# One layer of a hybrid RWKV-7 / RG-LRU block on one core: a score product moved up, a scan moved back, and the head norm's products and first gating regrouped

## The chip, the core and the metric

The kernel runs on one core of a Trainium2 chip. The time is the device time of one execution in microseconds (us). Profile times are microseconds on the clock of one profiled execution unless they are marked ns. The engines are PE (TensorE, the matrix products), DVE (VectorE), ACT (ScalarE), POOL (GpSimd) and SP (SyncE, which here only issues transfers). PEld is PE's weight load.

## What is computed

One layer at sequence length 512 and width 1024, all in float32. A normed input is projected by `w_in` (1024 x 4864) and feeds two mixers side by side; their outputs are gated, summed and projected, then follow a cross-attention and a gated conv-FFN. What the change touches lies in the two mixers and where they meet:

```python
def rwkv7_recurrence(r, decay, k, v, a, b):
    def step(state, inp):
        sa = jnp.einsum('bhij,bhj->bhi', state, a_t)
        state = (state * w_t[:, :, None, :] + sa[..., None] * b_t[:, :, None, :]
                 + v_t[..., None] * k_t[:, :, None, :])
        y_t = jnp.einsum('bhij,bhj->bhi', state, r_t)
...
    y = ((y - mean) * lax.rsqrt(var + LNX_EPS)).reshape(bsz, s, A_WIDTH) * lnx_g + lnx_b
    bonus = jnp.sum(r * k * r_k, axis=-1, keepdims=True) * v
    return (y + bonus.reshape(bsz, s, A_WIDTH)) * g
...
    u = xb * gate_x * mult
    _, h = lax.associative_scan(_lin_combine, (a, u), axis=1)
    return h * jax.nn.gelu(py.astype(jnp.float32))
...
        y_a = rwkv7_branch(...) @ w_branch_a[l]
        y_b = rglru_branch(...) @ w_branch_b[l]
        merged = (jax.nn.sigmoid(proj[..., cb2:cg1]) * y_a
                  + jax.nn.sigmoid(proj[..., cg1:]) * y_b)
        x = x + merged @ w_mix_out[l]
```

## The kernel before, in words

**Products in split float32.** Each float32 operand is split into a high part in a rounded format and a low part, and one product is made of three (`mm3`, L239): high by high, high by low, low by high. The weights stream from memory in tiles of 128 x 1024 (512 KB): SP issues the load (L169, four buffers), ACT casts the high part (`win_h`, L182, three buffers), DVE subtracts to get the low part (`win_l`, L183, three buffers), and PE uses both. A block of the input projection (`in_ps0` to `in_ps37`, 128 x 512) is 48 products of 128 x 256; three PSUM buffers serve these blocks. The same streaming serves `wbb` (weights of YB's branch) and `wba` (of the recurrence's branch).

**Order.** PE's order is the string `ORDER` (L44 on), which `Products.arrange` turns into dependencies: `in_ps25:42 sc3 in_ps25` puts 42 products of block 25, then all of `sc3`, then the rest of the block. On DVE, ACT and SP the build's scheduler chooses the order from the program order, priorities and the dependencies, so a change on PE moves instructions there too; each engine then runs its list in order.

**Recurrence.** It works in chunks of 64 steps. For each pair of heads, `prep2` makes the decayed keys `KBt` and the tile `AK` (L725 is the last write of `KBt`); `scores` (L753 on) makes the products `sc` of a chunk with itself, which DVE masks into `AK` (L767) and `BZ` (L768) and ACT copies into `BZ` (L769); four transfers per pair write the triangles to memory (`dM`, L774). There are four pairs, `sc0` to `sc3`. After the last pair two transfers bring all triangles back as `Nm` (L836), and a triangular inverse is built on DVE: 31 steps of a product `zz` (L843) and a sum into `Zt` (L845), each step's tile one column wider, up to 31 x 31, then a copy `Zn` (L846). `Zt` is cleared first (L837); it lies in the memory of the pool that `prep2` used, so the clearing has to wait for what still reads there, among it the transfer of `pr` to `dBo` (L733). While this inverse runs, PE works through the blocks 26 to 37 (`gate_block`) and the bonus sums `bo` (`bs` on DVE, L742).

**Chunk steps.** `chunk(c)` (c = 0 to 7) carries the state: PE makes `x`, DVE copies `Xs` (L949), PE makes `u`, ACT and DVE copy it into `UV` (L961, L962), PE makes `s` and `y`, DVE makes `Sn` (L978), adds it into the next `UV` (L982; `states[c]` is this instruction) and makes `SP` (L990). Between these steps PE works on the blocks 14 to 21.

**The other mixer** (`px_gates`, `px_scan`) makes four blocks of a gated linear scan in the same stretch: per block a DVE product (L1057), a one-column clear (L1058), a product (L1059) and the scan (L1060). Scans 2 and 3 are issued as a pair.

**The meeting point.** The recurrence's output is normed per head in two halves of time, each in two pairs (`group_norm`, tiles `gv0_0` to `gv1_1`): ACT squares, the square is split (`gv_h` on ACT L234, `gv_l` on DVE L235, in memory slots with the tag "xb"), PE sums it with `bonesr`, ACT takes the inverse root, DVE multiplies (L1019), scales and adds the bonus (L1022), gates (L1023) and splits into `ya`. YB's branch `yb_ps0` to `yb_ps7` (L1101 on) comes first on PE; each result is gated on DVE into `mB` (L1106) with a gate block `gb` loaded from memory (L1103, tags "ga", "gx", "st" in turn, two slots each). `yb_ps3` takes the PSUM buffer of `yb_ps0`, so it waits for `mB` of block 0. Then `ya_ps0` to `ya_ps7`, the mixing projection, attention and FFN follow.

Of the kernel before, what the change touches and what calls it, by code (L numbers as in the profile page):

```python
# [9 lines left out]
F32 = mybir.dt.float32  # L10
F32R = mybir.dt.float32r
AF = mybir.ActivationFunctionType
ALU = mybir.AluOpType
# [4 lines left out]
P = 128  # L18
T = 512
# [23 lines left out]

ORDER = """  # L44
in_ps4 in_ps5 psw0 psa0 in_ps0 in_ps1:6 ss0 in_ps1 in_ps8 in_ps9:6 sc0 in_ps9 psw1 psa1 ss1 in_ps6 in_ps7 in_ps2:12 sc1 in_ps2
psw2 psa2 in_ps3:10 ss2 in_ps3 in_ps10 in_ps11:36 sc2 in_ps11 in_ps22 psw3 psa3 ss3 in_ps23 in_ps24 in_ps25:42 sc3 in_ps25
in_ps26 in_ps27 in_ps28 bo0 in_ps29 bo1 in_ps30 bo2 in_ps31 bo3 in_ps32 in_ps33 in_ps34 in_ps35 in_ps36 in_ps37
in_ps14:40 zh0 in_ps14 in_ps15:14 zo0 zh16 in_ps15:16 zo16 in_ps15:8 vr0 ga0 in_ps15:6 x0 y0:8 kbr0 in_ps15
in_ps16:8 u0 vr1 gx0 in_ps16:12 s0 y0 kbr1 ga1 in_ps16:12 x1 y1:8 gx1 in_ps16:12 u1 vr2 in_ps16 in_ps17:8 s1 y1 kbr2
in_ps17:12 x2 y2:8 in_ps17:12 u2 vr3 in_ps17:12 s2 y2 kbr3 in_ps17 in_ps18:8 x3 y3:8 ga2 in_ps18:12 u3 vr4 gx2  # L50
in_ps18:12 s3 y3 kbr4 ga3 in_ps18:12 x4 y4:8 gx3 in_ps18 in_ps19:8 u4 vr5 in_ps19:12 s4 y4 kbr5 gv0_0 in_ps19:12 x5
y5:8 in_ps19:12 u5 vr6 gg0_0 in_ps19 in_ps20:8 s5 y5 kbr6 in_ps20:12 x6 y6:8 gv0_1 in_ps20:12 u6 vr7 gg0_1
in_ps20:12 s6 y6 kbr7 in_ps20 in_ps21:8 x7 y7:8 in_ps21:12 u7 in_ps21:12 y7 gg1_0 gg1_1 in_ps21 yb_ps0:18 yb_ps1:8 gv1_0 gv1_1 yb_ps1:10 yb_ps0 yb_ps1
yb_ps2 yb_ps3 yb_ps4 yb_ps5 yb_ps6 yb_ps7 ya_ps0 ya_ps1 ya_ps2 ya_ps3 ya_ps4 ya_ps5 ya_ps6 ya_ps7 mix_ps0
mix_ps1 mix_ps2 mix_ps3 mix_ps4 mix_ps5 mix_ps6 mix_ps7 q_ps0_0:32 rxc_ps q_ps0_0 q_ps0_1 q_ps1_0:24 sc_ps0_0
sc_ps0_1 q_ps1_0 q_ps1_1:4 sc_ps0_2 prT_ps0:2 q_ps1_1:8 sc_ps0_3 prT_ps0:2 q_ps1_1:18 prT_ps0 q_ps1_1:10 o_ps0
# [25 lines left out]
def hybrid_block_kernel(ctx: ExitStack, tc: tile.TileContext, xT_d, mT_d, pv_d, cst_d, win_d, wk_d, wv_d,  # L82
                        lup_d, gup_d, rga_d, rgx_d, wba_d, wbb_d, wmix_d, wq_d, wo_d, wfi_d, wfo_d, out_d):
    nc = tc.nc
    V, S = nc.vector, nc.scalar
# [144 lines left out]
    def sum_exact(ps, blocks, src, pool, tag, name, bufs=2, pin=lambda ins: ins):  # L230

        hi = pool.tile(list(src.shape), F32R, tag=tag, name=f"{name}_h", bufs=bufs)
        lo = pool.tile(list(src.shape), F32R, tag=tag, name=f"{name}_l", bufs=bufs)
        S.copy(hi, src)  # L234
        V.tensor_tensor(lo, src, hi.bitcast(F32), ALU.subtract)  # L235
        pin(PE.matmul(ps, blocks, hi, start=True, stop=False))
        PE.matmul(ps, blocks, lo, start=False, stop=True)
# [47 lines left out]
    bonesr = cp.tile([P, P], F32R, name="bonesr")  # L285
# [73 lines left out]
    with tc.tile_pool(name="p0", bufs=1, reuse_waits="tile") as p0:  # L359
# [102 lines left out]
        st = stream(wv_d, "wv", at=OFF)  # L462
# [162 lines left out]
    tp = tp_ctx.enter_context(tc.tile_pool(name="tp", bufs=1, reuse_waits="tile"))  # L625
# [195 lines left out]
    for k, i in enumerate(IN_REST[NEARLY:NMID]):  # L821
        gate_block(i - 22)
        j = k + NEARLY - 6
# [81 lines left out]
    yT = vT  # L905
# [32 lines left out]
    states, uvs = [], []  # L938
# [61 lines left out]
    ya2 = pa.tile([P, 2, 4, T], F32R, tag="AR", name="ya2")  # L1000


    def group_norm(hf, jp, ps, psg):
        n = T // 2
        ts = slice(hf * n, (hf + 1) * n)
        js = slice(2 * jp, 2 * jp + 2)
        nm = f"{hf}_{jp}"
        bo = ch.tile([P, 2, n], F32, tag="bo", name=f"bo{nm}", bufs=2)
        nc.scalar.dma_start(bo, dBo[js, :, ts].rearrange("j p t -> p j t"))
        y2 = ch.tile([P, 2, n], F32, tag="y2", name=f"y2{nm}", bufs=2)  # L1010
        S.activation(y2, yT[:, js, ts], AF.Square)
        p3 = ps.rearrange("p (j t) -> p j t", j=2)
        sum_exact(ps, bonesr, y2.rearrange("p j t -> p (j t)"), tp, "xb", f"gv{nm}")
        tab.rsqrt(y2, p3, 1.0 / HD, eps[:, 1:2])
        g3 = psg.rearrange("p (j t) -> p j t", j=2)
        for i in range(2):
            j = 2 * jp + i
            PE.matmul(g3[:, i, :], gup[:, j * P:(j + 1) * P], sgx[:, ts], start=True, stop=True)
        V.tensor_tensor(y2, yT[:, js, ts], y2, ALU.mult)  # L1019
        for i in range(2):  # L1020
            j = 2 * jp + i
            V.scalar_tensor_tensor(y2[:, i, :], y2[:, i, :], par("lnx_g", j), bo[:, i, :], ALU.mult, ALU.add)  # L1022
        V.tensor_tensor(yT[:, js, ts], y2, g3, ALU.mult)  # L1023
# [28 lines left out]
    def px_scan(b, xb, ga, gx, behind):  # L1052
        tab(ga, ga, AF.Exp, scale=c8[:, b:b + 1])
        tab(gx, gx, AF.Ln, bias=eps[:, 2:3])
        tab(gx, gx, AF.Exp, scale=0.5)
        with tc.issue_after(behind.ins) if behind is not None else nullcontext():
            V.scalar_tensor_tensor(gx, ga, 1.0, gx, ALU.add, ALU.mult)  # L1057
        V.memset(gx[:, 0:1], 1.0)  # L1058
        V.tensor_tensor(xb, xb, gx, ALU.mult)  # L1059
        V.tensor_tensor_scan(YB[:, b, :], ga, xb, 0.0, ALU.mult, ALU.add)  # L1060
# [9 lines left out]
    for i in IN_REST[NMID:]:  # L1070
        if i < 18:
            pair.append(px_gates(i - 14))
            if len(pair) == 2:
                for p in pair:
                    px_scan(*p, {1: states[2]}.get(p[0]))
                pair = []
        elif i < 22:
            if i == 18:
                for jp in range(2):
                    group_norm(0, jp, rw_ps(f"gv0_{jp}", prg, "rg"), rw_ps(f"gg0_{jp}", prg, "rg"))  # L1080
            py_block(i - 18)
        else:
            gate_block(i - 22)
# [10 lines left out]
    mB = big.tile([P, KB, T], F32, tag="act16_1", name="mB")  # L1094
# [4 lines left out]
            V.tensor_tensor(yb2[:, 1, b, :], yb, yb2[:, 0, b, :].bitcast(F32), ALU.subtract)  # L1099
    ub = Units(wbb_d, "wbb", at=OFF)  # L1100
    for m in range(KB):  # L1101
        gb = tp.tile([P, T], F32, tag=("ga", "gx", "st")[m % 3], name=f"gb{m}", bufs=2)
        nc.sync.dma_start(gb, dG[8 + m])  # L1103
        psb = mm_ps(f"yb_ps{m}")
        dense(psb, ub, lambda kb: (yb2[:, 0, kb, :], yb2[:, 1, kb, :]), 4)
        V.tensor_tensor(mB[:, m, :], psb, gb, ALU.mult)  # L1106
    pq_ctx.close()
    tp_ctx.close()

# [550 lines left out]
```

## Time and profile before

| | before |
|---|---|
| time, median of 3 runs | 878.45 us (873.0 to 879.46) |
| profiled execution | 876.36 us, span 874.6 us, granted clock 0.997 |
| PE busy | 853.7 us (98%) |
| DVE busy | 677.3 us (77%) |
| ACT busy | 511.3 us (58%) |
| POOL busy | 132.6 us (15%) |
| DMA | 201.60 MB, mean 231 GB/s |

A row of the timeline has a start, a duration, the engine, the line, the operation with output and inputs, a count, and in brackets the idle time of the engine before it with what ended it; the duration of a row with a count covers the first start to the last end. Matmuls overlap, so the step from one row's start to the next tells more than a duration. `SPq` and `ACTq` rows are the issue of a transfer, not the transfer; the time to landing stands in the view of a tile. The waits of an engine are summed per line and releaser. Names of tiles leave the number of the buffer out: `in_ps` is any of the blocks.

### The profile page before, as it was taken

How to read it: one execution, taken by the hardware profiler on the slowest of the kernel's cores; microseconds unless marked ns; L12 is line 12 of the kernel's file. 1: busy time of each engine (PE TensorE's matmuls, PEld its weight loads, DVE VectorE, ACT ScalarE, POOL GpSimd, SP SyncE). 2: the span in 40 equal slices, each digit the busy share in tenths (PEclk: the TensorE clock that was granted, in tenths of full speed). 3: DMA queues.
4: the chain of work that ended last, by engine and by line, in shares of the span. 5: the costliest groups of instructions: out<-in, count | busy, mean ns of one | idle time of the engine just before them, and what ended most of it. 6: DMA issues, size and time to landing. Idle time of an engine off the chain costs nothing.

```text
span 874.6 us, 19292 instructions
## 1 busy us (share of the span) xinstructions
PE 853.7 (98%) x7884; PEld 825.9 (94%) x7884; DVE 677.3 (77%) x1096; ACT 511.3 (58%) x786; POOL 132.6 (15%) x163
## 2 busy tenths in 40 slices
PE   9999999999999999999999999999999999999996
PEld 8899999998988888999999899999999999999996
DVE  6896988759836787585575568799888888999774
ACT  7777666534337667234464457666666566768563
POOL 0111123021002221001122211111111111111100
PEclk9999999999999999999999999999999999999998
DMA  8888799687676898648887858999999999998953
GB/s 288 309 286 201 191 239 219 217 234 229 197 191 133 198 241 204 200 161 234 222 237 175 194 146 194 259 274 291 285 258 288 306 280 291 261 291 224 299 178 97
DMA packets 97576, 201.60 MB, mean 231 GB/s; under 512 B 19600, under 2 KB 30992, under 8 KB 97424
## 3 DMA queue, kind: packets, MB, share of 16 engines
q1 hardware_dynamic: 62240, 118.57, 40.5%
q0 software_dynamic: 25504, 67.38, 37.3%
q10 hardware_dynamic: 9744, 14.42, 5.0%
q8 instruction: 62, 1.02, 0.4%
q14 instruction: 26, 0.21, 0.1%
HBM read 188.54 MB, written 78.12 MB: 305 GB/s over the span
## 4 chain that ended last, share of the span: by engine, by line
PE 74%; DVE 13%; ACT 6%; DMA 4%; issue 3%; DVEq 0%; ACTq 0%; SPq 0%
PE fx_ps L97 14%; PE in_ps L97 12%; PE fyz_ps L97 10%; PE ox_ps L97 7%; PE oyz_ps L97 5%; PE co_ps L97 5%; PE mix_ps L97 4%; PE q_ps L97 4%; PE yb_ps L97 2%; DVE win_l L183 2%; PE v_ps L97 2%; PE o_ps L97 1%; DVE zz L843 1%; PE sc_ps L97 1%; DVE Zt L845 1%
## 5 line engine op out<-in xcount | busy, mean ns | idle before, releaser
L97 PE MATMUL in_ps<-hT,win_h 128*128 128x256 f32 x1216 | 211.8, 278 | 0.0
L97 PEld LDWEIGHTS in_ps<-hT,win_h 128*128 128x128 f32 x1216 | 184.8, 188 | 3.6 <-issue 1.9
L97 PE MATMUL in_ps<-hT,win_l 128*128 128x256 f32 x608 | 174.1, 286 | 3.5 <-DVE win_l L183 3.5
L97 PEld LDWEIGHTS in_ps<-hT,win_l 128*128 128x128 f32 x608 | 114.2, 188 | 7.4 <-DVE win_l L183 4.7
L206 ACT CAST wfi_h<-wfi_r 128x1024 fp32r<-128x1024 f32 x77 | 80.9, 1051 | 68.6 <-PE fyz_ps L97 22.8
L563 POOL DMA_DIRECT2D dS<-in_wfi x66 | 66.7, 1039 | 332.9 <-PE in_ps L97 136.8
L207 DVE TENSOR_TENSOR wfi_l<-wfi_r,wfi_h 128x1024 fp32r<-128x1024 f32 x77 | 94.1, 1222 | 19.8 <-ACT wfi_h L206 19.8
L599 POOL DMA_DIRECT2D dOs<-in_wfo x54 | 39.8, 799 | 169.1 <-PE fx_ps L97 66.1
L97 PE MATMUL fx_ps<-hq,wfi_h 128*128 128x256 f32 x352 | 61.2, 276 | 0.0
L97 PE MATMUL fx_ps<-hr,wfi_h 128*128 128x256 f32 x352 | 61.1, 276 | 0.0
L97 PE MATMUL fyz_ps<-hq,wfi_h 128*128 128x256 f32 x352 | 61.1, 276 | 0.0
L183 DVE TENSOR_TENSOR win_l<-win_r,win_h 128x1024 fp32r<-128x1024 f32 x38 | 46.3, 1222 | 18.3 <-ACT win_h L182 18.1
L97 PE MATMUL ox_ps<-go,wfo_h 128*128 128x256 f32 x352 | 59.9, 276 | 0.0
L182 ACT CAST win_h<-win_r 128x1024 fp32r<-128x1024 f32 x38 | 39.8, 1047 | 30.1 <-PE in_ps L97 24.8
L1467 DVE TENSOR_TENSOR wfo_l<-wfo_r,wfo_h 128x1024 fp32r<-128x1024 f32 (+1 forms) x39 | 47.3, 1216 | 11.0 <-ACT wfo_h L1466 10.9
L1466 ACT CAST wfo_h<-wfo_r 128x1024 fp32r<-128x1024 f32 (+1 forms) x39 | 40.4, 1037 | 24.6 <-PE ox_ps L97 8.7
L97 PEld LDWEIGHTS fx_ps<-hr,wfi_h 128*128 128x128 f32 x352 | 53.0, 188 | 0.2 <-ACT sn L1402 0.2
L97 PEld LDWEIGHTS fx_ps<-hq,wfi_h 128*128 128x128 f32 x352 | 53.2, 188 | 0.0
L97 PEld LDWEIGHTS ox_ps<-go,wfo_h 128*128 128x128 f32 x352 | 53.1, 188 | 0.0
L97 PEld LDWEIGHTS fyz_ps<-hq,wfi_h 128*128 128x128 f32 x352 | 53.0, 188 | 0.0
L97 PE MATMUL fyz_ps<-hq,wfi_l 128*128 128x256 f32 x176 | 48.7, 277 | 0.6 <-DVE wfi_l L207 0.6
L97 PE MATMUL fx_ps<-hq,wfi_l 128*128 128x256 f32 x176 | 48.6, 276 | 0.0
(392 smaller groups left out, 2331.2 us busy)
## 6 DMA issues: line engine op xcount, KB each, us to landing
dS<-in_wfi POOLq DMA_DIRECT2D x66, 512.0 KB, 8.0
wfi_r<-dS SPq DMA_DIRECT2D x44, 512.0 KB, 6.9
win_r<-in_win SPq DMA_DIRECT2D x38, 512.0 KB, 5.2
wfi_r<-in_wfi SPq DMA_DIRECT2D x33, 512.0 KB, 7.2
dS<-dS POOLq DMA_DIRECT2D x22, 512.0 KB, 5.6
dOs<-in_wfo POOLq DMA_DIRECT2D x12, 512.0 KB, 8.4
wk_r<-in_wk SPq DMA_DIRECT2D x8, 512.0 KB, 5.1
wv_r<-in_wv SPq DMA_DIRECT2D x8, 512.0 KB, 4.9
```

The lines of the kernel that those rows point to most:

```text
L97: return self.log(out, nc.tensor.matmul(out, *args, **kw))
L182: casts.append(S.copy(hi[:, o:o + n], raw[:, o:o + n]))
L183: lows[name, g] = V.tensor_tensor(lo[:, o:o + n], raw[:, o:o + n], hi[:, o:o + n].bitcast(F32), ALU.subtract)
L206: S.copy(hi, raw)
L207: V.tensor_tensor(lo, raw, hi.bitcast(F32), ALU.subtract)
L563: return lambda: nc.gpsimd.dma_start(s(out), src, **kw)
L599: yield lambda k=k, w=w, src=src: nc.gpsimd.dma_start(dO[n, m][:, k * P:(k + w) * P], src, **kw)
L843: steps.append(V.tensor_tensor(t3, Zt[:, s + 1:, s + 1:], Nm[:, s:s + 1, s + 1:].to_broadcast([P, n, n]), ALU.mult))
L845: V.tensor_reduce(Zt[:, s + 1:, s:s + 1], t3, AX.X, ALU.add)
L1466: S.copy(hi[:, :n], raw[:, :n])
L1467: V.tensor_tensor(lo[:, :n], raw[:, :n], hi[:, :n].bitcast(F32), ALU.subtract)
```

## The change

It has five parts. First, the 16 x 2 score products `sc3` of the last pair stand after 36 products of block 25 in PE's order, where they stood after 42. Second, the norm's four products `gv1_0` and `gv1_1` stand together between `yb_ps0:18` and `yb_ps1:18`; they stood between the first 8 and the next 10 of `yb_ps1`. Third, the split tiles of `gv1_1` take slots of tag "gx". Fourth, the scan of block 3 is issued behind `states[5]`. Fifth, the gate tiles `gb` take their tags in pairs, and a dependency on VectorE places the norm's multiplication of the second pair (`norms[-1]`) behind `mB` of block 0. No instruction's size is changed, and no product is added or removed.

```diff
-psw2 psa2 in_ps3:10 ss2 in_ps3 in_ps10 in_ps11:36 sc2 in_ps11 in_ps22 psw3 psa3 ss3 in_ps23 in_ps24 in_ps25:42 sc3 in_ps25
+psw2 psa2 in_ps3:10 ss2 in_ps3 in_ps10 in_ps11:36 sc2 in_ps11 in_ps22 psw3 psa3 ss3 in_ps23 in_ps24 in_ps25:36 sc3 in_ps25
...
-in_ps20:12 s6 y6 kbr7 in_ps20 in_ps21:8 x7 y7:8 in_ps21:12 u7 in_ps21:12 y7 gg1_0 gg1_1 in_ps21 yb_ps0:18 yb_ps1:8 gv1_0 gv1_1 yb_ps1:10 yb_ps0 yb_ps1
+in_ps20:12 s6 y6 kbr7 in_ps20 in_ps21:8 x7 y7:8 in_ps21:12 u7 in_ps21:12 y7 gg1_0 gg1_1 in_ps21 yb_ps0:18 gv1_0 gv1_1 yb_ps1:18 yb_ps0 yb_ps1
...
+    norms = []
...
-        sum_exact(ps, bonesr, y2.rearrange("p j t -> p (j t)"), tp, "xb", f"gv{nm}")
+        sum_exact(ps, bonesr, y2.rearrange("p j t -> p (j t)"), tp, "gx" if hf and jp else "xb", f"gv{nm}")
...
-        V.tensor_tensor(y2, yT[:, js, ts], y2, ALU.mult)
+        norms.append(V.tensor_tensor(y2, yT[:, js, ts], y2, ALU.mult))
...
-                    px_scan(*p, {1: states[2]}.get(p[0]))
+                    px_scan(*p, {1: states[2], 3: states[5]}.get(p[0]))
...
-        gb = tp.tile([P, T], F32, tag=("ga", "gx", "st")[m % 3], name=f"gb{m}", bufs=2)
+        gb = tp.tile([P, T], F32, tag=("ga", "gx", "st")[m // 2 % 3], name=f"gb{m}", bufs=2)
...
-        V.tensor_tensor(mB[:, m, :], psb, gb, ALU.mult)
+        out = V.tensor_tensor(mB[:, m, :], psb, gb, ALU.mult)
+        if m == 0:
+            tc.add_manual_dep(norms[-1].ins, out.ins.name, mybir.DependencyInfo(
+                mybir.DependencyClass.NoSync, mybir.DependencyReason.DATA), reason="order on VectorE")
```

What the scheduler made of it, at three places. In the rows a minus is the order before, a plus the order of the change, and a row without either stands in both. The first is DVE at the scores of the last pair and the start of the inverse (`win_l20` to `win_l28` are low parts of streamed weights, `blo` the split of the bonus terms):

```order
-L837 MEMSET Zt_2620 128x1024
 L767 TENSOR_TENSOR AK_760<-sc3_0_0_2056,cst_76 64x512
 L768 TENSOR_TENSOR BZ_757<-sc3_0_0_2056,cst_76 64x4x64
...
-L183 TENSOR_TENSOR win_l20_2356<-win_r20_2353,win_h20_2355 128x1024
 L768 TENSOR_TENSOR BZ_757<-sc3_1_0_2072,cst_76 64x4x64
 L767 TENSOR_TENSOR AK_760<-sc3_1_1_2073,cst_76 64x512
 L768 TENSOR_TENSOR BZ_757<-sc3_1_1_2073,cst_76 64x4x64
 L820 TENSOR_TENSOR blo0_2099<-bt0_2103,bhi_2098 128x512
+L183 TENSOR_TENSOR win_l20_2356<-win_r20_2353,win_h20_2355 128x1024
 L820 TENSOR_TENSOR blo1_2100<-bt1_2107,bhi_2098 128x512
+L837 MEMSET Zt_2620 128x1024
```

The clearing of `Zt` and one weight split went from ahead of and between the masks to behind them. In the inverse that follows, the weight splits stand some steps further back; its end reads, on DVE:

```order
 L845 TENSOR_REDUCE Zt_2620<-zz_2622 128x27
-L183 TENSOR_TENSOR win_l27_3637<-win_r27_3634,win_h27_3636 128x1024
 L843 TENSOR_TENSOR zz_2622<-Zt_2620,Nm_2619 128x784
 L845 TENSOR_REDUCE Zt_2620<-zz_2622 128x28
 L843 TENSOR_TENSOR zz_2622<-Zt_2620,Nm_2619 128x841
+L183 TENSOR_TENSOR win_l27_3637<-win_r27_3634,win_h27_3636 128x1024
 L845 TENSOR_REDUCE Zt_2620<-zz_2622 128x29
-L183 TENSOR_TENSOR win_l28_3695<-win_r28_3692,win_h28_3694 128x1024
 L843 TENSOR_TENSOR zz_2622<-Zt_2620,Nm_2619 128x900
 L845 TENSOR_REDUCE Zt_2620<-zz_2622 128x30
 L843 TENSOR_TENSOR zz_2622<-Zt_2620,Nm_2619 128x961
+L183 TENSOR_TENSOR win_l28_3695<-win_r28_3692,win_h28_3694 128x1024
```

Both splits went back by one and a half of the 31 steps. On SP the four `dM` transfers went ahead of the load `win_r24`, and both `Nm` ahead of `win_r25`, which stood between them. The third place is DVE at chunk step 5, of the change, where `Sn5` to `SP5` are the state update (`gx3`, `xb3` and the `YB` row behind `Xs6` are scan 3; before, all of scan 3 and `wbb_l0` stood ahead of `Sn5`):

```order
L1025 TENSOR_TENSOR vT_759<-y20_0_4133,gg0_0_4130 128x2x256
L978 TENSOR_TENSOR Sn5_3334<-s5_3310,PC_761 128x256
L183 TENSOR_TENSOR wbb_l0_4483<-wbb_r0_4480,wbb_h0_4482 128x1024
L982 TENSOR_TENSOR UV6_3298<-Sn5_3334,SP4_3262 64x256 x2
L990 TENSOR_TENSOR SP5_3338<-UV6_3298,PC_761 64x256 x2
L1059 SCALAR_TENSOR_TENSOR gx3_4109<-ga3_4108,gx3_4109 128x512
L949 COPY Xs6_3351<-x6_3342 128x256
L1060 MEMSET gx3_4109 128x1
L1061 TENSOR_TENSOR xb3_4098<-xb3_4098,gx3_4109 128x512
L1062 SCALAR_TENSOR_TENSOR YB_2615<-ga3_4108,xb3_4098 128x512
L1021 TENSOR_TENSOR y20_1_4153<-vT_759,y20_1_4153 128x512
L962 COPY UV6_3298<-u6_1_3363 64x256
```

Lines of the change are two higher here than before. Scan 3 now stands between the state update of step 5 and the copy of `u6`. At the meeting point `gv1_1_l` went from behind the last `yb` split to right behind `gv1_0_l`, and `mB` of block 0 from behind both pairs' norms to behind the first pair's (L1022), with `mB` of block 1 still behind the second's; the norm's `gv1_1_h` on ACT stands right behind `gv1_0_h`, and the inverse root of `gv1_0` starts ahead of the last `yb` cast. On SP the loads `gb2` and `gb3` stand behind `wba_r2`; `gb2` stood behind `wba_r1`, and `gb3` ahead of `wba_r0`.

## The prediction

> **What bounds the kernel now.** I read the busy shares of the table above first, then PE's waits by releaser, then the chain of waits, then the timelines of the three places that these name.
>
> ```profile
> PE in_ps L97 <- DVE win_l L183: 3.5, 6, 1.0
> PE yb_ps L97 <- DVE mB L1106: 1.5, 1, 1.5
> PE zh L97 <- issue: 1.4, 1, 1.4
> PE x L97 <- DVE UV L982: 0.8, 1, 0.8
> PE gv L97 <- ACT gv_h L234: 0.7, 1, 0.7
> PE gv L97 <- DVE gv_l L235: 0.3, 1, 0.3
> 181.94 9.24 DMA Nm<-dM
> ...
> 223.82 10.96 PE in_ps L97 x94
> ```
>
> PE is busy for 98% of the span, so a change pays only through PE's pauses. The five rows with a DVE or ACT releaser are the pauses at the places of the change, 6.8 us together. [...] The last two lines are pieces of the chain in order of time: it runs once through a transfer of 9.24 us, the one that opens the triangular inverse, and 94 block products in a row take 10.96, 0.117 each.
>
> **Part 1, the scores six products earlier.** DVE around the scores of the last pair, with PE and SP:
>
> ```profile
> 164.31 1.40 DVE L725 TENSOR_TENSOR KBt<-pk,L 64x512 f32<-64x512 f32 x2
> 169.42 0.91 DVE L837 MEMSET Zt<- 128x1024 f32 x1 [2.93 <-DMA dBo<-pr]
> 170.36 0.69 DVE L767 TENSOR_TENSOR AK<-sc,cst 64x512 f32<-64x512 f32 x1
> 175.45 0.43 DVE L768 TENSOR_TENSOR BZ<-sc,cst 64x256 f32<-64x256 f32 x1
> 191.31 0.16 DVE L843 TENSOR_TENSOR zz<-Zt,Nm 128x1 f32<-128x1 f32 x1 [6.78 <-DMA Nm<-dM]
> ```
> ```profile
> 165.59 2.29 PE L97 MATMUL sc<-AK,KBt 64*128 64x128 f32 x32
> 175.26 2.36 SPq L774 DMA_DIRECT2D dM<-BZ  x4
> 180.67 0.48 SPq L836 DMA_DIRECT2D Nm<-dM  x1
> 181.19 0.59 SPq L169 DMA_DIRECT2D win_r<-in_win  x1
> 181.94 1.27 SPq L836 DMA_DIRECT2D Nm<-dM  x1
> DMA to landing us min/median/max: 3.7/6.5/9.2
> ```
>
> The products of `sc` alternate between two halves of `KBt`, and the second is written at 164.31 + 1.40 = 165.71. PE cannot start sooner than it does now, so six block products at 0.117 now run behind the scores: a loss of 0.7. What it buys is not on PE but on DVE. `Zt`'s clearing waits 2.93 us for the transfer of `pr` while the finished scores wait behind it. With the clearing (0.91) and one weight split (1.2) behind the masks, `AK` starts when the first scores are out, about 167.0, and four pairs of masks at 0.69 + 0.35 end at 171.2 instead of 175.9. `dM` is issued from 170.6 to 172.9, some 4.7 earlier. The second `Nm` followed 4.3 us after the end of that issue (177.6 to 181.9), which now gives 177.2, and the load `win_r25` (181.19) no longer stands between the two. The last row has the time from issue to landing of the two `Nm`; on 177.2 it gives a start T of the inverse between 180.9 and 186.4; DVE is itself ready at about 180, after the other splits. I take **T = 183**, a little under the median, because the 9.2 belongs to the transfer that had a fresh weight load ahead of it.
>
> What does T have to be? During the inverse DVE is the bound: its 31 products alone take 15.8 us, its sums as much, and the weight splits stand between them.
>
> ```profile
> L843 DVE TENSOR_TENSOR zz<-Zt,Nm 128x1 f32<-128x1 f32 (+30 forms) x31 | 15.8, 510 | 7.7 <-DMA Nm<-dM 6.8
> 222.55 1.22 DVE L183 TENSOR_TENSOR win_l<-win_r,win_h 128x1024 fp32r<-128x1024 f32 x1
> 222.78 0.39 PE L97 MATMUL in_ps<-hT,win_h 128*128 128x256 f32 x2
> 223.82 0.39 PE L97 MATMUL in_ps<-hT,win_l 128*128 128x256 f32 x1 [0.65 <-DVE win_l L183]
> 225.69 1.04 DVE L843 TENSOR_TENSOR zz<-Zt,Nm 128x841 f32<-128x841 f32 x1
> ```
>
> At 223.82 the step from the row before is 1.04 where two products take 0.23: 0.81 lost, 0.16 more than the idle time. Six pauses of 3.5 in sum so lose 3.5 + 6 x 0.16 = 4.5. `win_l27` (222.55) ends 32.5 us behind the inverse's start. In the new order `win_l22` (1.2) and a step and a half, three instructions of about 1.04 (225.69), stand ahead of it as well, so it ends at about T + 37. PE got there at 223.0; without its four earlier pauses (2.7 with their share of 0.16) and 0.7 later it would want the split at 221.0. So all 4.5 vanish if T is below about 184, and from there each microsecond of T costs one. Because the splits stand further back than before, the new order needs its early start. At T = 183 the part gives -4.5 + 0.7 = **-3.8**; bounds -3.8 and, at T = 186.4, -1.4.
>
> [...]
>
> **Part 4, scan 3 behind the state update.** DVE and PE at step 5, and the undisturbed `x` and `y` of the step before:
>
> ```profile
> 313.59 0.43 DVE L962 COPY UV<-u 64x256 f32<-64x256 f32 x1
> 315.06 1.22 DVE L1060 TENSOR_TENSOR_SCAN YB<-ga,xb 128x512 f32<-128x512 f32 x1
> 316.57 1.22 DVE L183 TENSOR_TENSOR wbb_l<-wbb_r,wbb_h 128x1024 fp32r<-128x1024 f32 x1
> 317.82 0.42 DVE L978 TENSOR_TENSOR Sn<-s,PC 128x256 f32<-128x256 f32 x1
> 318.75 0.86 DVE L982 TENSOR_TENSOR UV<-Sn,SP 64x256 f32<-64x256 f32 x2
> 315.16 0.69 PE L97 MATMUL s<-UV,KBr 128*64 128x64 f32 x16
> 319.22 1.07 PE L97 MATMUL x<-UV,AK 128*64 128x64 f32 x15 [0.80 <-DVE UV L982]
> 320.75 0.50 PE L97 MATMUL gv<-gv_h,bonesr 128*128 128x512 f32 x1
> 309.15 0.69 PE L97 MATMUL x<-UV,AK 128*64 128x64 f32 x16
> 310.24 0.39 PE L97 MATMUL in_ps<-hT,win_l 128*128 128x256 f32 x1
> ```
>
> `s` is out at about 315.9, but `Sn` starts at 317.82 behind the scan and the split. Now the order behind `UV` (314.0) is two scalings, a gating, `Sn` at 315.9, the split to 317.5, `UV` to 318.4. PE is due at `x` at 318.42, so it waits no more. `x` and `y` took 319.22 + 1.53 and the pause 0.80, together 2.33, against 1.09 from 309.15 to 310.24: **-1.2**. Bounds: -0.8, the idle alone, and -1.2. The scan goes to 320.3 to 322.2, ahead of the copy of `u6`; by PE's order `s6` comes about 5.6 us behind `x` (324.0), so it is covered by 0.7 us, and without that cover it would cost what the scan is late.
>
> **Parts 2, 3 and 5, the norm's products and the first gating.**
>
> ```profile
> 341.44 0.39 PE L97 MATMUL gv<-gv_h,bonesr 128*128 128x512 f32 x1
> 343.85 0.28 PE L97 MATMUL yb_ps<-yb,wbb_l 128*128 128x256 f32 x1
> 348.97 0.28 PE L97 MATMUL yb_ps<-yb,wbb_l 128*128 128x256 f32 x1
> 350.75 0.47 PE L97 MATMUL yb_ps<-yb,wbb_h 128*128 128x256 f32 x2 [1.50 <-DVE mB L1106]
> 349.91 0.69 DVE L1106 TENSOR_TENSOR mB<-yb_ps,gb 128x512 f32<-128x512 f32 x1
> ```
>
> Four norm products of 512 columns, twice a block product's 0.117, take 0.9; from 341.44 to 343.85 they take 2.41, so 1.5 is lost there. The second `gv_h`, on which PE waits, comes late because its slots are those of the first pair, which PE reads until about 341.9. In "gx" slots it follows the first on ACT at once, and its split too: the 1.5 vanish. Ten more products ahead of the rest of `yb_ps0` cover the last `yb` cast, which now stands behind one inverse root and ends, split and all, when PE arrives (within 0.1). `yb_ps3` lost 350.75 - 348.97 - 0.11 = 1.67 waiting for `mB` of block 0. That gating now follows the first pair's norm on DVE and ends some 2 us before `yb_ps3` is due. What is late next is `mB` of block 1, for `yb_ps4`: between the two gatings stand a gating, a multiplication, a split, two scalings, an `ya` split and a gating (0.6 + 0.6 + 1.2 + 0.9 + 0.6 + 0.6) and its own 0.69, so it ends about 0.55 behind PE's arrival. Sum: -1.5 - 1.67 + 0.55 = **-2.6**. Bounds: -3.2 if that wait is nothing, -1.5 if it takes the place of the old one. The `gb` loads change order on SP: `gb2` now stands behind `wba_r2`, but is due only with `yb_ps5`, some ten microseconds later.
>
> **The sum** is -3.8 - 1.2 - 2.6 = -7.6. All of it is taken off PE before 352 us; from there on PE has few pauses and nothing in the order changes, so it should reach the end. On the profiled execution, 876.36 - 7.6 = 868.8 (span 867.0). The four times shown, with the profiled one, have a mean of 876.8, which gives 869.2; the median of 878.45 would give 870.9. I take **869.5**.
>
> **The rivals.** (a) `Nm` takes the long landing. [...] Against it: the load that was issued between is now behind both. At T = 186.4 to 187.4, 9.2 on an issue that also slips by one, the first part keeps 0.4 to 1.4, the sum is about -4.7, and the time 872.1. (b) The gating wait moves on: `mB` of block 1 is held by ACT's inverse root and PE waits at `yb_ps4` as long as it did at `yb_ps3`. For it: it stands behind eight DVE instructions; against it: what they read is made before the first gating ends. Sum -3.8 - 1.2 - 1.5 = -6.5, time 870.3. (c) The other side: the inverse starts no earlier than before, because `dM` issued into busier queues lands late and `Nm` after it. The splits now stand further back, so PE's pauses grow by one for each microsecond of T beyond 184; from T = 191.6 on the loss is larger than all three gains. With 9.2 for `dM` and 9.2 for `Nm` on 172.9, and the 1.27 that the second `Nm` took to issue, T is 192.6, the loss 8.6 against 7.6, and the time 877.8. Against it: `dM` took 4.3 us on the same queue before. (d) The change does more than said: if the paced splits also free the wait at `zh` (1.4), -9.0 and 867.8. Against it: that wait is between `zo`, its copy and `zh16`, all moved together.
>
> **How the numbers follow.** The forecast 0.50, (a) 0.22, (b) 0.13, (c) 0.07, (d) 0.08. The range has to hold the base too: the fastest run of before, 873.0, less 7.6 is 865.4, and the slowest, 879.46, less the 4.7 of (a) is 874.8; it goes from 865 to 876.5, which stops just short of (c). About 1%, 8.8 us, is what a measurement of this kernel can tell from no change, since its runs spread from 873.0 to 879.46. The forecast lies at 0.87%, so it passes 1% only in part of its cases, and in (d): faster 0.34, same 0.62, slower 0.04.
>
> **What would show it.** Right: `zz` starts before 184, and no `win_l` row stands among PE's waits between 190 and 240; `Zt`'s clearing has no wait for `pr`; `x` at step 6 has no pause; the four `gv` rows follow at about 0.23; `yb_ps3` has no pause and `yb_ps4` one of about half a microsecond. A start of `zz` behind 184 with `win_l` pauses is (a), behind 191 (c). Wrong altogether would be a pause of PE behind 352 that before had not, as large as the sum.

## The result, and the profile after

| | before | change |
|---|---|---|
| median of 6 runs each | 877.78 us (873.0 to 879.75) | 868.29 us (865.9 to 870.8) |
| ratio | | 0.9895, interval 0.9864 to 0.9927 |
| profiled execution | 876.36 us, span 874.6 us | 865.9 us, span 864.1 us |

The change is faster by 1.05%, 9.5 us between the medians; the forecast was 869.5, from a sum of 7.6 us. In a later measurement it took 866.96 (866.47 to 867.69) against 879.96, ratio 0.9856 (0.9827 to 0.9885). One of the 17 runs of before in that measurement, 1421.69 us at a granted clock of 0.556, is left out of the ratio.

PE's waits by releaser; the columns are us in total, times, longest:

```profile
PE sc L97 <- DVE KBt L725: 0.8, 2, 0.4
...
PE zh L97 <- issue: 0.3, 1, 0.3
PE yb_ps L97 <- DVE mB L1108: 0.3, 1, 0.3
```

The rows of `win_l`, `x` and `gv` are gone, `yb_ps` kept 0.28 of 1.5, and `sc` has two pauses, 0.8 together, where before had one of 0.5. The chain of waits, which ran through the landing of `Nm` before, is now almost PE alone (before: PE 74%, DVE 13%, DMA 4%):

```profile
PE 89%; DVE 5%; ACT 3%; DMA 1%; issue 1%; DVEq 0%; ACTq 0%
```

DVE's timeline around the scores of the last pair, at the end of the inverse and at `Sn` of step 5, in the form start, duration, engine, line, operation, and the idle time before it:

```profile
163.65 1.40 DVE L725 TENSOR_TENSOR KBt<-pk,L 64x512 f32<-64x512 f32 x2
166.17 0.69 DVE L767 TENSOR_TENSOR AK<-sc,cst 64x512 f32<-64x512 f32 x1 [0.34 <-PE sc L97]
169.98 0.43 DVE L768 TENSOR_TENSOR BZ<-sc,cst 64x256 f32<-64x256 f32 x1
173.03 0.91 DVE L837 MEMSET Zt<- 128x1024 f32 x1 [0.16 <-DVE blo L820]
181.78 0.16 DVE L843 TENSOR_TENSOR zz<-Zt,Nm 128x1 f32<-128x1 f32 x1 [2.20 <-DMA Nm<-dM]
217.10 1.22 DVE L183 TENSOR_TENSOR win_l<-win_r,win_h 128x1024 fp32r<-128x1024 f32 x1
...
309.45 0.42 DVE L978 TENSOR_TENSOR Sn<-s,PC 128x256 f32<-128x256 f32 x1 [0.78 <-PE s L97]
```

The masks run from 166.17 to 170.41 without a break, the clearing behind them no longer waits for `pr`, and the inverse starts at T = 181.78 where it started at 191.31. `win_l27` (217.10) ends at 218.32, T + 36.5. `Sn` waits for PE now, where it stood behind scan 3. SP in the same stretch, and the landing of the two `Nm`:

```profile
169.85 2.14 SPq L774 DMA_DIRECT2D dM<-BZ  x4
172.29 0.89 SPq L169 DMA_DIRECT2D win_r<-in_win  x1
174.79 1.12 SPq L836 DMA_DIRECT2D Nm<-dM  x2
```
```profile
DMA to landing us min/median/max: 4.9/5.6/6.2
```

PE at the scores, at `win_l27`, at `x` of step 6, at the norm's products and at `yb_ps4`:

```profile
164.38 0.48 PE L97 MATMUL sc<-AK,KBt 64*128 64x128 f32 x2
165.19 2.02 PE L97 MATMUL sc<-AK,KBt 64*128 64x128 f32 x30 [0.33 <-DVE KBt L725]
...
219.70 0.28 PE L97 MATMUL in_ps<-hT,win_l 128*128 128x256 f32 x1
...
311.90 0.69 PE L97 MATMUL x<-UV,AK 128*64 128x64 f32 x16
...
332.76 0.39 PE L97 MATMUL gv<-gv_h,bonesr 128*128 128x512 f32 x1
...
333.45 0.39 PE L97 MATMUL gv<-gv_l,bonesr 128*128 128x512 f32 x1
...
342.98 0.48 PE L97 MATMUL yb_ps<-yb,wbb_h 128*128 128x256 f32 x2 [0.28 <-DVE mB L1108]
```

PE reaches the product that needs `win_l27` at 219.70, 1.38 us behind its end. `x` follows without a pause, the four `gv` stand 0.23 apart, `yb_ps3` has no row with a pause, and `yb_ps4` waits 0.28.

**Where the time came from.** Both kernels have 7884 products on PE, in nearly one order. The start of the n-th product in the trace of before, less that of the n-th in the trace of the change, is a ledger: it changes only where one of the two loses time.

| place | ledger steps to | step | predicted |
|---|---|---|---|
| products before 127 us | +0.7 | +0.7 | 0 |
| `sc3` | 0.0 | -0.7 | -0.7 |
| six `win_l` pauses | +5.35 | +5.35 | +4.5 |
| inside `zh16` | +6.4 | +1.1 | 0 |
| `x` of step 6 | +7.7 | +1.25 | +1.2 |
| `gv` | +9.25 | +1.5 | +1.5 |
| `yb_ps3` | +11.0 | +1.8 | +1.67 |
| `yb_ps4` | +10.5 | -0.5 | -0.55 |

From `yb_ps4` to the last product it stays at 10.5. The first row and `zh16` lie where no instruction moved; experiments below show that they vary between runs of one kernel. Without them the ledger gives 8.7: 4.65 of part 1, 1.25 of part 4, 2.8 of parts 2, 3 and 5.

### The profile page after: what moved, and what is told of

Read it like the earlier page. It is cut to its first block, busy times and chain, and to the rows that moved or that the text cites. A ratio compares the mean times of both kernels' runs of the same rounds, so it can differ in the third digit from the quotient of the medians.

```text
span 864.1 us, 19296 instructions
## 1 busy us (share of the span) xinstructions
PE 850.7 (98%) x7884; PEld 825.0 (95%) x7884; DVE 676.8 (78%) x1096; ACT 511.5 (59%) x786; POOL 132.6 (15%) x163
## 3 DMA queue, kind: packets, MB, share of 16 engines
q8 instruction: 62, 1.02, 0.4%
## 4 chain that ended last, share of the span: by engine, by line
PE 89%; DVE 5%; ACT 3%; DMA 1%; issue 1%; DVEq 0%; ACTq 0%
PE in_ps L97 21%; PE fx_ps L97 14%; PE fyz_ps L97 10%; PE ox_ps L97 7%; PE oyz_ps L97 5%; PE co_ps L97 5%; PE mix_ps L97 5%; PE q_ps L97 4%; PE k_ps L97 3%; PE v_ps L97 3%; PE o_ps L97 1%; PE yb_ps L97 1%; PE sc_ps L97 1%; PE y L97 1%; PE sc L97 1%
```

## The experiments

The account to be tested: where `Zt` is cleared, ahead of the last masks or behind them, sets T, and T sets PE's pauses at the weight splits; parts 4 and 2, 3, 5 each remove their own pause. Its rivals: six products earlier are needed for it; the load between the two `Nm` makes them late; the gains share one cause, so that a part alone gives nothing; `zh16` belongs to the change.

| kernel | median us (range, runs) | ratio to before, interval | T | lost at `win_l` |
|---|---|---|---|---|
| part 1 alone | 871.8 (870.98 to 873.52, 6) | 0.9913, 0.9886 to 0.994 | 182.63 | 0 |
| part 4 alone | 877.29 (871.84 to 881.8, 12) | 0.9971, 0.9945 to 0.9998 | 195.90 | 10.0 |
| parts 2, 3, 5 | 874.92 (870.63 to 881.67, 12) | 0.9948, 0.9922 to 0.9974 | 194.27 | 8.4 |
| clearing behind, 42 | 867.25 (866.49 to 867.71, 5) | 0.9858, 0.983 to 0.9887 | 183.33 | 0 |
| clearing ahead, 36 | 875.31 (869.38 to 880.83, 12) | 0.9938, 0.9912 to 0.9965 | 190.21 | 3.5 |
| before, `Nm` ahead of the load | 878.27 (875.84 to 880.89, 10) | 0.9991, 0.9967 to 1.0016 | 192.73 | 7.6 |
| the change again | 866.96 (866.47 to 867.69, 5) | 0.9856, 0.9827 to 0.9885 | 182.52 | 0 |
| clearing behind, both gatings early | 866.36 (866.15 to 867.55, 5) | 0.9852, 0.9821 to 0.9883 | 183.74 | 0 |

The last two columns are of each kernel's profiled execution; "lost" is the ledger's step from the scores to the end of the inverse, against the change.

**Part 1 alone.** Before, with one number of the order changed:

```diff
-... in_ps23 in_ps24 in_ps25:42 sc3 in_ps25
+... in_ps23 in_ps24 in_ps25:36 sc3 in_ps25
```

> Before with the first part alone (scores after 36 products). Theory A: the scores cost PE 0.7, the masks on DVE end some 4.7 us sooner, the inverse starts at 181 to 183 instead of 191.3, and the six pauses for win_l, which the trace puts at 5.3 from start to start, are gone: 4.7 us less, or 5.8 if the pause at zh shrinks from 1.4 to 0.3 here too. The pauses at x (0.8), gv (1.0) and yb_ps3 (1.5) stay. About 872. Rival B: PE's sooner arrival is given back at those later waits, since the state chain sets the pace there: under 2 us less.

Measured 871.8 against 879.4. DVE's timeline and PE's waits:

```profile
182.63 0.16 DVE L843 TENSOR_TENSOR zz<-Zt,Nm 128x1 f32<-128x1 f32 x1 [1.53 <-DMA Nm<-dM]
```
```profile
PE yb_ps L97 <- DVE mB L1106: 1.5, 1, 1.5
...
PE x L97 <- DVE UV L982: 0.8, 1, 0.8
...
PE gv L97 <- ACT gv_h L234: 0.7, 1, 0.7
```

No `win_l` row is left, and the other pauses stand as before. One number in PE's order moved the clearing and the weight splits on DVE and the transfers on SP. By the medians the part is worth 7.6 us (5.3 to 10.0 by the interval), more than the 4.65 of the ledger, and the runs spread over 2.5 us where before's spread over 8.3.

**Part 4 alone, and parts 2, 3 and 5 alone.**

```diff
-                    px_scan(*p, {1: states[2]}.get(p[0]))
+                    px_scan(*p, {1: states[2], 3: states[5]}.get(p[0]))
```

> Before with the fourth part alone (scan 3 behind the state update of step 5). Theory A: the pause at x of step 6 goes and 1.2 us with it; win_l, gv and yb_ps3 keep their pauses; 876.5 for a before of 877.8. Rival B: PE comes 1.2 sooner to the norm's products and waits as much longer for ACT there: no gain.

The second is the change with `in_ps25:42 sc3` and without that line.

> The change without its first and fourth part (scores after 42 products, scan 3 where it was). Theory A: the two pauses at gv (1.5 from start to start) go, that at yb_ps3 (1.7) becomes one of about 0.5 at yb_ps4: 2.7 us less. Rival B: the first gating only hands its wait to the second, as long as before: 1.5 less.

Each removed its own pause and no other: part 4 that at `x` (1.3 in the ledger), parts 2, 3, 5 those at `gv` and `yb_ps3`, with the 0.28 at `yb_ps4`. By the medians they are worth 2.1 and 4.5, intervals 0.2 to 4.8 and 2.3 to 6.9. With the 7.6 of part 1 the medians add up to 14.2, near the 13.0 of the change's second measurement, so there is no common cause. What was not expected is in the stretch that these kernels share with before. The first product with `win_l22` in the trace of part 4 alone, PE's waits, and windows of 4 us (busy time of PE, PEld, DVE, ACT, POOL, then the granted clock, DMA share and GB/s):

```profile
202.41 0.39 PE L97 MATMUL in_ps<-hT,win_l 128*128 128x256 f32 x1 [4.84 <-DVE win_l L183]
```
```profile
PE in_ps L97 <- DVE win_l L183: 7.2, 4, 4.8
```
```profile
200.00:204.00 4.00, 1.58 (x9) 1.59 (x10) 3.76 (x10) 2.34 (x3) 0.72 (x1) 0.86 0.47 159
204.00:208.00 4.00, 4.00 (x28) 4.00 (x28) 3.76 (x10) 0.03 (x2) 0.00 (x0) 0.72 0.67 235
```

T is 195.90 here, and PE loses 10.0 us: 7.2 idle, some 0.3 more for each of four restarts, and 1.7 at a lowered clock (4 us at 0.86 and 4 at 0.72). The profile of parts 2, 3, 5 shows the same in less. In the five profiles of an order in which the clearing stands ahead of all the masks the loss is 3.5, 5.35, 7.6, 8.4 and 10.0 us. That fits the spread of the runs of before; its profiled execution, with 5.35, was one of the milder.

**The clearing behind the masks, with the scores at their old place.** The change with `in_ps25:42 sc3`, and a dependency in place of the earlier scores (`masks` collects the instructions of L767 and L768):

```diff
-... in_ps25:36 sc3 in_ps25
+... in_ps25:42 sc3 in_ps25
-        V.memset(Zt, 0.0)
+        clear = V.memset(Zt, 0.0)
+        tc.add_manual_dep(clear.ins, masks[-1].ins.name, mybir.DependencyInfo(
+            mybir.DependencyClass.NoSync, mybir.DependencyReason.DATA), reason="order on VectorE")
```

> The change with the scores after 42 products as before, but with the clearing of Zt put behind the last pair's masks on DVE by a dependency. Theory A: what the first part bought is the place of the clearing, not the six products; the inverse starts at 181 to 183, no pause for win_l, and the 0.7 that the scores' wait cost is saved: 0.5 to 0.8 us faster than the change, about 867.6. Rival B: the sooner scores matter too; the inverse starts later than 184 and pauses for win_l come back, so it is not faster than the change.

DVE's timeline:

```profile
166.69 0.69 DVE L769 TENSOR_TENSOR AK<-sc,cst 64x512 f32<-64x512 f32 x1 [0.34 <-PE sc L97]
...
173.59 0.91 DVE L839 MEMSET Zt<- 128x1024 f32 x1 [0.16 <-DVE blo L822]
183.33 0.16 DVE L847 TENSOR_TENSOR zz<-Zt,Nm 128x1 f32<-128x1 f32 x1 [2.85 <-DMA Nm<-dM]
```

867.25 us, no `win_l` pause. The six products earlier are not what is needed: they cost 0.7 on PE and only led the scheduler to put the clearing behind. The two kernels get their early T by different shares: here the second `Nm` is issued at about 179.1, 2.8 us earlier than before's, and lands in 4.1 us instead of 9.2; in the change it is issued 6.5 us earlier and lands in 6.2.

**The clearing ahead of the masks, with the scores early.** The reverse. The first attempt:

```diff
+        tc.add_manual_dep(masks[-8].ins, clear.ins.name, mybir.DependencyInfo(
+            mybir.DependencyClass.NoSync, mybir.DependencyReason.DATA), reason="order on VectorE")
```

> The change (scores after 36 products) with the clearing of Zt put back ahead of the last pair's masks by a dependency. Theory A: the clearing's place is the cause: it waits for pr again, the masks end near 175, the inverse starts between 190 and 196, and the pauses for win_l are back, 5 to 11 us; 873 to 879 and a wide spread of the runs. Rival B: the sooner scores are the cause: the inverse starts before 185 and the time stays near 868.

This missed its aim. The dependency held one pair of masks, the scheduler ran the other three ahead of the clearing, and it set the weight splits earlier in the inverse. The clearing no longer waited for `pr`. T was 188.37, and still no block of the input projection paused for `win_l` (867.89, 867.38 to 868.59); one pause of 0.52 for a split came later, at `zo`, with a step of 1.2 in the ledger. It does show that a limit on T holds for one placing of the splits only. The second attempt holds all eight masks:

```diff
+        for mask in masks[-8:]:
+            tc.add_manual_dep(mask.ins, clear.ins.name, mybir.DependencyInfo(
+                mybir.DependencyClass.NoSync, mybir.DependencyReason.DATA), reason="order on VectorE")
```

> The change (scores after 36 products) with the clearing of Zt ahead of all eight masks of the last pair; the scheduler then puts the transfers and splits where they were before, too. Theory A: the clearing's place is what the first part bought; it waits for pr, the masks end at 175 to 177, the inverse starts between 190 and 196, PE pauses 5 us or more for win_l and pays 0.7 at the scores: 5 to 9 us slower than the change, with runs spread over 6 us or more. Rival B: the sooner scores are enough: the inverse starts before 186 and the time is within 1 us of the change.

DVE's timeline and PE's waits:

```profile
169.50 0.91 DVE L839 MEMSET Zt<- 128x1024 f32 x1 [2.96 <-DMA dBo<-pr]
170.44 0.69 DVE L769 TENSOR_TENSOR AK<-sc,cst 64x512 f32<-64x512 f32 x1
...
190.21 0.16 DVE L848 TENSOR_TENSOR zz<-Zt,Nm 128x1 f32<-128x1 f32 x1 [5.68 <-DMA Nm<-dM]
```
```profile
PE in_ps L97 <- DVE win_l L183: 2.4, 3, 1.0
```

875.31 against 866.96 for the change on the same chip, 8.4 us, though the scores still start early. The waiting clearing, the late masks, the late T and the pauses are back together, and so is the spread (11.5 us). The profiled execution was a mild one, 872.47 us: it lost 3.5 us at `win_l`, less than the 5 that were expected, and 1.6 at a lowered clock in `zh16`; where the slower runs lose the rest no trace shows. With the kernel above, it shows the clearing's place to be the cause of part 1's gain, together with the orders of splits and loads that the scheduler derives from it, which no run separates.

**`Nm` ahead of the load that stood between.** Before, with `win_r25` behind both `Nm` on SP (`back` collects the issues of L836):

```diff
+                if (name, g) == ("win", 25):
+                    tc.add_manual_dep(ins.ins, back[-1].ins.name, mybir.DependencyInfo(
+                        mybir.DependencyClass.NoSync, mybir.DependencyReason.DATA), reason="order of the loads")
```

> Before, with both transfers of Nm ahead of the load win_r25 on SP's queue (which stood between them) and all else the same. Theory A: the second Nm was slow because of the fresh 512 KB load ahead of it; it lands within 4 to 6.5 us like the first, the inverse starts at 185.5 to 188.5 instead of 191 to 196, and at most 2 us of the pauses for win_l are left: 3 to 5 us faster than before. Rival B: the traffic of the other queues (bonus terms, gates, feed-forward copies) holds it; it takes 9 to 12 again, the inverse starts at 191 or later, no gain.

SP's timeline and the landing:

```profile
182.37 2.79 SPq L841 DMA_DIRECT2D Nm<-dM  x2
185.25 0.55 SPq L171 DMA_DIRECT2D win_r<-in_win  x1
```
```profile
DMA to landing us min/median/max: 7.9/8.6/9.2
```

No difference in time, and `Nm` still takes 7.9 to 9.2 with nothing of SP between. The load between the two is not to blame. Windows of before and of the change (the last two columns are DMA share and GB/s):

```profile
168.00:172.00 4.00, 4.00 (x36) 4.00 (x36) 2.54 (x4) 0.46 (x3) 0.00 (x0) 1.00 0.07 24
172.00:176.00 4.00, 4.00 (x37) 4.00 (x37) 3.88 (x8) 2.41 (x5) 0.66 (x1) 1.00 0.33 87
```
```profile
168.00:172.00 4.00, 4.00 (x37) 4.00 (x37) 3.94 (x7) 3.02 (x6) 1.72 (x2) 1.00 0.14 26
172.00:176.00 4.00, 4.00 (x38) 4.00 (x37) 2.68 (x6) 1.44 (x2) 0.88 (x2) 1.00 0.81 243
```

From 168 to 172 the DMA engines stand nearly idle in both (0.07 and 0.14). From 172 to 176 they are at 0.33 in before, whose masks end only at 175.9, and at 0.81 in the change. From 176 on both are full (0.87 to 1.08 in each window up to 188). The issues of `dM` between 168 and 196, of before and of the change, with the median time to landing last:

```profile
dM<-BZ SPq DMA_DIRECT2D x4, 32.0 KB, 4.4
```
```profile
dM<-BZ SPq DMA_DIRECT2D x4, 32.0 KB, 2.5
```

Even these small transfers take 1.9 us longer in before. So the total traffic does not tell why `Nm` lands sooner in the change. The packet records of the traces point to one queue, `q0 software_dynamic` of the page, which between 168 and 196 moves 1.57 MB, the size of the three copies `dS` that POOL issues. From the issue of the second `Nm` to the last landing, its packets fill 3% of the DMA engines' time in the kernel with the clearing behind and the scores at 42, where the second `Nm` lands in 4.1 us; 26% in the change (6.2); 37% in before (9.2); 49% in this kernel (7.9, the first 9.2); 54% with part 4 alone (12.6). No run moved those copies alone, so this is a likely cause, not a shown one.

**The change without single pieces.** Without the dependency of `mB` on the norm:

```diff
-        if m == 0:
-            tc.add_manual_dep(norms[-1].ins, out.ins.name, ...
```

> The change without the dependency of the fifth part: mB of block 0 goes behind the second pair's multiplication, the split wbb_l3 and one scaling. Theory A: yb_ps3 waits again, 1.0 to 1.6 us, yb_ps4 no longer; nothing else moves, so the time from the norm's products to yb_ps5 is 0.6 to 1.1 longer than in the change. Rival B: the pairing of the gb slots did it, not the dependency: no pause at yb_ps3.

And without the "gx" slots:

```diff
-        sum_exact(..., "gx" if hf and jp else "xb", f"gv{nm}")
+        sum_exact(..., "xb", f"gv{nm}")
```

> The change with the split of gv1_1 back in the xb slots. Theory A: the second gv_h waits until PE has read the first pair, the pauses at gv (together 1.2 to 1.6) are back, now ahead of yb_ps1; the rest stays. Rival B: bringing the four products together was enough, since more of yb_ps1 now follows: under 0.4.

PE's timeline of the first, then of the second:

```profile
344.14 0.48 PE L97 MATMUL yb_ps<-yb,wbb_h 128*128 128x256 f32 x2 [2.40 <-DVE mB L1108]
```
```profile
338.99 0.49 PE L97 MATMUL gv<-gv_h,bonesr 128*128 128x512 f32 x1 [2.65 <-ACT gv_h L234]
339.88 0.51 PE L97 MATMUL gv<-gv_l,bonesr 128*128 128x512 f32 x1 [0.40 <-DVE gv_l L235]
```

One run each: 869.85 and 874.0, where before had 880.01. Both pauses came where expected, but at 2.40 and 2.65 instead of 1.0 to 1.6: the moved products bring PE there sooner than the second pair's work is ready, so each piece alone is needed more than it was in before. In the ledger the first costs 2.1 and the second 4.7, each net of the wait at `yb_ps4` that goes with it; part of the second is lost at a lowered clock (below).

**The pause in `zh16`.** The change with two copies of 1 MB that nothing reads, issued by ACT at the start of that stretch, to see whether traffic lengthens the pause:

```diff
+            if i0 == 0 and e == 0:
+                for t in range(2):
+                    extra = nc.scalar.dma_start(dX[t], wfi_d[2 * t:2 * t + 2])
```

> The change plus two transfers of 1 MB from weights to an unused place in memory, issued on ACT right behind the first copy of Hs, so that the DMA engines are busy when PE is in the middle of zh16. They change no result. Theory A: the pause in zh16 (1.4 before, 0.3 in the change) is PE waiting for its next instructions, which come over the same DMA engines; the instruction fetch of 16 KB lands later and the pause grows from 0.3 to at least 1.2. Rival B: the pause belongs to the copies between zo and zh16; it stays at 0.3 to 0.5.

And the change once more, unaltered:

> The change itself once more, beside the run above and before. Theory A: about 868.3, 9 to 11 us under before, runs within 5 us of each other; the inverse starts at 181 to 184 with no pause for win_l; the pause in the middle of zh16, 0.3 in its first profile, lies anywhere from 0.1 to 1.4, since kernels with the same order at this place showed all of that. Rival B: the pause in zh16 is a property of the kernel and is 0.3 again.

The run with the traffic took 872.31. Its pause was 1.22, but 1.25 in the unaltered change:

```profile
247.75 0.63 PE L97 MATMUL zh<-ZA,BZ 32*32 32x32 f32 x28 [1.25 <-issue]
```

So the traffic shows nothing, and the 1.1 us that the ledger put at `zh16` were a matter of the execution. The pause stands ahead of the same product in 13 of the 14 traces, with no semaphore to wait for, from 0.16 to 1.39 us long. What its length goes with can be read from the packet records of the queue `q8` on the page (packets, MB, share of the DMA engines' time):

```profile
q8 instruction: 62, 1.02, 0.4%
```

Its 62 packets have 16 KB each. In all 13 traces the 16th packet ends 1.24 to 1.59 us before the pause ends (at 251.22 and 252.71 in before, at 244.76 and 246.28 in the change), whether PE came to this product 0.02 or 1.30 us behind the end of the packet. In the fourteenth, the kernel that held one pair of masks, PE came more than 3 us behind it, and there is no pause. So the pause fits theory A, a wait for instructions. The added copies did not test it: in that run the packet took 0.93 us, within the 0.88 to 1.11 of the others. Against the profile of before, this second profile of the change (867.69 us, span 865.9) is 8.7 ahead in all, as much as the ledger's 8.7.

**The clearing behind and both first gatings early.** The kernel with the clearing behind the masks, with one condition changed:

```diff
-        if m == 0:
+        if m < 2:
             tc.add_manual_dep(norms[-1].ins, out.ins.name, ...
```

> The kernel with scores after 42 products and the clearing of Zt behind the masks, and the gatings of blocks 0 and 1 both ahead of the second pair's norm. Theory A: the pause of 0.5 at yb_ps4 goes as well and no new one comes, since the second pair's norm has ten microseconds until ya_ps0: 866.7, against 867.25 for the one without. Rival B: the split wbb_l3 behind them is late for yb_ps6, or mB of block 1 waits for PE and holds DVE up: no gain or 0.5 slower.

866.36 us, no pause at `yb_ps3` or `yb_ps4`. It beats before clearly (0.9852, 0.9821 to 0.9883). It undercuts the change's 868.29 and 866.96, but those come from other measurements, the second on another chip, and the intervals overlap: a gain over the change, 1.2 us by the trace (0.7 at `sc3`, 0.5 at `yb_ps4`), is not shown by the times.

## Why the prediction was right

The forecast of 869.5 stands 1.2 us above the measured 868.29, and the range of 865 to 876.5 holds every run of the change. The gain of 1.05%, with 0.7% to 1.4% as its interval, lies on the bound of about 1% that the prediction drew between "same" and "faster", and it had given the larger chance, 0.62, to "same". The time was forecast better than the gain: 7.6 us against 9.5 here and 13.0 later. By its steps:

- **T.** Predicted 183, measured 181.78 and, in the second profile, 182.52. In the first profile PE was 0.7 ahead of before already at 127 us, so on before's clock T is 182.5. The chain held link by link: `AK` at 166.17 (167.0 predicted), masks out at 170.41 (171.2), `dM` from 169.85 to 171.99 (170.6 to 172.9). `Nm` was issued sooner than reckoned, because `dM` landed in 2.5 us; the prediction carried over the 4.3 us of the congested order.
- **The limit on T.** "Below about 184" fits: `win_l27` ended at T + 36.5 (T + 37 predicted), and PE wanted it 1.38 later, so the limit in this execution is 183.2, or 183.9 on before's clock.
- **The six pauses: the mis-sized term.** Predicted 4.5, measured 5.35 in the ledger. The restart was costed as 0.16 over the idle time, from the step to the first product behind one pause, 0.81. In the ledger this same pause costs 0.94, since the next products lose a further 0.13; over all six the restart is (5.35 - 3.54) / 6 = 0.30. The starts in before's trace show where some of it lies: the product after the first one behind each of the six pauses comes 0.22 us later, where two in the stream stand 0.11 to 0.12 apart. Beyond that the term was taken from one execution with T = 191.3. By the medians part 1 is worth 7.6; the profiles with a later T and a larger loss fit that, though the slower runs of before have no trace. "Each microsecond of T costs one" was said of the new order beyond 184, and no run of that order came there. In the orders with the clearing ahead, the loss goes from 3.5 at 190.21 to 10.0 at 195.90, 1.14 per microsecond, with 1.7 of the 10.0 at a lowered clock.
- **`sc3`.** 0.7 predicted, 0.7 measured; it shows as a second `sc` pause of 0.33 and as later products.
- **Part 4.** 1.2 predicted, 1.25 in the ledger. `Sn` had a wait of 0.78 for PE ahead of it, so DVE was ready, and the scan behind the update delayed nothing.
- **Parts 2, 3 and 5.** 1.5, 1.67 and -0.55 predicted; 1.5, 1.8 and -0.5 measured. The wait of `yb_ps4` on the second gating came as said, which rules out rival (b). Here DVE's order could be summed up instruction by instruction.
- **The rivals.** (a) fell: `Nm` landed in 4.9 and 6.2, where the rival gave it the 9.2 of before. Over all the kernels the same transfer took 3.5 to 12.6, and no run shows what sets this; the landing did not follow the total traffic: from 176 to 184 the DMA share was 1.05 and 1.08 in the change, and from 180 to 188, in the flight of before's `Nm`, 0.87 and 1.02. (c) did not come about in the change; what it describes, late landings and so a late T, is what slows before and every kernel here that clears ahead of all the masks. (d) seemed to come true in the first profile, with 0.32 at `zh16` instead of 1.39; the second profile, with 1.25, takes it back.
- **The base.** The sum was made against a mild execution of before. Later medians of before were 879.4 to 880.0, and in the measurement of both the gain was 13.0 instead of 9.5. The forecast time was still near, because what is left when the pauses of one execution are taken off that same execution moves little: 876.36 less the ledger's 8.7 is 867.7, as the second profile took. The prediction did not argue this; that its time held against a slower base is partly luck. That the rest of the program passes the gain on held: no step of the ledger lies behind `yb_ps4`, and in the second profile only one of 0.4, at the mixing projection.

## What to carry to other kernels

An instruction that has to wait for an outgoing transfer, here the clearing of reused memory, belongs behind the work that feeds the critical transfers: its own wait of 3 to 4.6 us went with 3.5 to 10 us lost on PE, and with most of the spread between runs. When a schedule is left to a planner, a small edit elsewhere can move such an instruction by accident; name it and pin it with a dependency, as the kernel with the clearing behind the masks does. Cost a pause at its whole step on the engine, and look at several executions before sizing a term that hangs on when a transfer lands.

## What the runs showed of the hardware

**Behind some pauses PE's granted clock was lower.** No profile of before or of the change has a window with a lowered clock at these places (1.00 in each). In other kernels some longer pauses have a lowered clock behind them. Windows of the kernel without "gx" slots (behind its 2.65 us) and of the kernel without the gating's dependency (around its 2.40 us):

```profile
340.00:344.00 4.00, 4.00 (x21) 3.95 (x22) 2.00 (x4) 1.83 (x3) 0.00 (x0) 0.57 1.08 266
```
```profile
340.00:344.00 4.00, 1.74 (x16) 1.54 (x14) 4.00 (x8) 1.20 (x2) 0.00 (x0) 1.00 1.10 282
344.00:348.00 4.00, 3.86 (x34) 3.89 (x35) 2.48 (x4) 1.01 (x2) 0.00 (x0) 1.00 0.66 229
```

The clock was lowered behind pauses of 2.65, 3.28 and 4.84 us; with those of 2.40 and, with `Nm` ahead of the load, 2.38 it stayed at 1.00. Each time it cost 1.7 us of clock by the windows of 4 us: 4 x 0.43 behind the 2.65 and behind the 3.28, 4 x (0.14 + 0.28) behind the 4.84. No run varied the length or the place of a pause alone, so what a pause needs to lower the clock is not shown.

**Among small products it was lower behind shorter pauses.** In the stretch of 32 x 32 products it was lowered behind a pause of 1.22 us in the kernel with the copies:

```profile
246.00:250.00 4.00, 2.78 (x85) 2.63 (x79) 2.61 (x3) 1.62 (x3) 0.00 (x0) 0.73 0.71 283
250.00:254.00 4.00, 4.00 (x68) 3.77 (x68) 2.78 (x5) 0.30 (x1) 0.00 (x0) 0.50 0.42 130
254.00:258.00 4.00, 4.00 (x43) 3.53 (x38) 0.85 (x2) 0.99 (x3) 0.00 (x0) 0.50 0.53 153
```

That cost some 4.2 us in the ledger; with the 0.99 of the next window the windows lose 5.1 us of clock, and in two of them the clock was 0.50. The same happened behind pauses of 0.94 and 1.06 in the kernel without "gx" slots (0.77 and 0.80 in two windows) and in that with the clearing ahead (0.74 and 0.83), for 1.7 us of clock each, and not behind 1.25 in the change or 1.22 in the kernel without the gating's dependency (1.00 in each window from 246 to 258). Here the length alone does not decide; what does is not shown, and that the small products are the reason was not tried by itself.

**The same transfer of 256 KB landed in 3.5 to 12.6 us.** The 3.5 is from the kernel with the clearing ahead, the 12.6 from part 4 alone. Taking the load beside it out of its way in SP's queue did not help (7.9 and 9.2); the longer landings go with the packets of POOL's copies, as said above.
